# The norm sums of an RWKV-7 recurrence: transposed spreading through TensorE against broadcast reads from a DRAM scratch

## The chip, the cores and the metric

The kernel runs on one core of one Trainium2 chip. The metric is the device time of one execution in microseconds (us). A core has five engines that run side by side, each with its own instruction queue in order: PE (TensorE, matmuls; its weight loads are listed as PEld), DVE (VectorE), ACT (ScalarE), POOL (GpSimd) and SP (SyncE, here only a DMA issuer). PSUM is the memory that matmuls write; SBUF is the working memory with 128 partitions.

## The reference

One step of a one-layer decoder trunk, in fp32, for 1024 prompt tokens and 8 x 8 sample tokens. What matters here is the recurrent branch, with 8 heads of 64 channels:

```python
kk = heads(k * k_k)
kk = kk * rsqrt(sum(kk * kk, over the head) + 1e-12)
...
y, wkv_new = wkv7_scan(state, r, decay, k, v, kk, a)      # delta rule, token by token
mean = mean(y, over the head)
var = mean(square(y - mean), over the head)
y = (y - mean) * rsqrt(var + GN_EPS) * ln_w + ln_b
bonus = sum(rh * kh * r_k, over the head) * vh
y = (y + bonus) * g
```

Each token and head has four such sums over 64 channels: of kk squared, of y, of y squared, and of the bonus. Around it stand one large projection `P = h @ w_in`, a pooling branch, the merge with `w_out`, and an MLP.

## The kernel before, in words

Channels lie on the partitions and the 1088 tokens along the free axis. Two heads share one tile of 128 partitions, so there are four head pairs, f = 0 to 3. A sum over a head is therefore a sum over 64 partitions, which no elementwise engine does. TensorE does it, in two ways:

- `bones`: a matmul with a 128x128 matrix of two blocks of ones gives the head's sum on all its 64 partitions at once. It is used for the mean in `post` (L1204) and in `bonus` (L814), in chunks of 512/288/288 or 364/362/362 tokens.
- `rinv` (L385) and `spread` (L406): nine matmuls of 128 tokens each give the sums with the tokens on partitions (128x2). ACT takes the square root (L396, which loads its table first), DVE the reciprocal (L397), ACT copies the result out to 64 columns per head (L401) and touches Tanh (L403, which loads that table back). `spread` then transposes the 128x128 blocks back, one PE transpose for each block of 128 tokens (L211), and DVE multiplies from PSUM (L720 for kk, L1216 for y).

The sequence for a head pair is `front` (kk's norm and the low-rank terms of decay and `a`), `burst`, `scores` (with `unit` and `bonus`), then `inverse`, `level` and `affine` for the chunks' triangular systems, the chain of chunk states, `sample` and `post` (group norm and gate). `heads` runs `inverse`, `level` and `affine` of f together with a filler: `post` of f-1 followed by `front` of f+1. The inverse is a loop on DVE (L923, L925) that ends with transposes (L933); its result goes through `hv,hv` and `iv,hv` matmuls with an eviction on DVE between them (L954).

The order of PE is written out by hand: generators yield a number of nanoseconds or a condition, and `Pace` puts their matmuls into a dense background stream. In this phase (77 to 752 us of the profile) that stream is the projection `w_in`: 34 blocks of 72 matmuls, each with a 128x128 weight against 362 or 364 tokens. A weight is split into a high and a low half, and each product is three matmuls, written `mm<-hx,whi` and `mm<-hx,wlo`. The splitting (`wlo<-wraw,whi`) is DVE work (L228). The other engines' orders come from a scheduler that estimates times; an engine that reaches an instruction early waits there, and everything behind it waits too. After 752 us stand the merge, the output projection and the MLP, which the change does not touch.

## Time and profile before

| | |
|---|---|
| median of the runs | 1617.38 us (1616.26 to 1618.33, 3 runs) |
| profiled execution | 1622.76 us, span 1621.0 us |
| busy share of the span | PE 97%, PEld 91%, DVE 63%, ACT 45%, POOL 22% |
| phase with the recurrence, 77 to 752 us | PE busy 660.34 of 675.00 us, DVE 389.81, ACT 277.94, POOL 56.98 |
| rest, 752 to 1621 us | PE busy 854.66 of 869.00 us |
| mean granted TensorE clock | 0.989 |

Busy time is the time in which an engine had an instruction under way. Matmuls are pipelined, so their durations in the rows overlap; what a matmul costs the stream is read from the distance between starts, not from its duration. "Idle before, releaser" names what an engine waited for. PEclk is the share of full clock that TensorE was granted.

### The profile page before, as it was taken

How to read it: one execution, taken by the hardware profiler on the slowest of the kernel's cores; microseconds unless marked ns; L12 is line 12 of the kernel's file. 1: busy time of each engine (PE TensorE's matmuls, PEld its weight loads, DVE VectorE, ACT ScalarE, POOL GpSimd, SP SyncE). 2: the span in 40 equal slices, each digit the busy share in tenths (PEclk: the TensorE clock that was granted, in tenths of full speed). 3: DMA queues.
4: the chain of work that ended last, by engine and by line, in shares of the span. 5: the costliest groups of instructions: out<-in, count | busy, mean ns of one | idle time of the engine just before them, and what ended most of it. 6: DMA issues, size and time to landing. Idle time of an engine off the chain costs nothing.

```text
span 1621.0 us, 35482 instructions
## 1 busy us (share of the span) xinstructions
PE 1576.7 (97%) x14331; PEld 1472.5 (91%) x14331; DVE 1020.1 (63%) x1747; ACT 734.6 (45%) x1491; POOL 358.1 (22%) x464
## 2 busy tenths in 40 slices
PE   6999999999999999999999999999999999999997
PEld 3999878997898889879989999999999999999997
DVE  5685574756565636334635587776555677787866
ACT  5543343354334434432325475554445765553323
POOL 3301210020001000101513322333233343521221
PEclk9999999999999999899999999999999999999998
DMA  9334314333413242836874465667666965674313
GB/s 336 108 120 157 134 58 132 108 101 112 152 67 114 90 144 91 296 121 210 328 273 166 143 215 199 205 231 257 223 204 227 321 201 183 199 265 154 101 40 111
DMA packets 123380, 279.43 MB, mean 172 GB/s; under 512 B 16816, under 2 KB 31152, under 8 KB 123216
## 3 DMA queue, kind: packets, MB, share of 16 engines
q1 hardware_dynamic: 107856, 228.52, 41.2%
q0 software_dynamic: 9312, 32.41, 6.0%
q10 hardware_dynamic: 6048, 16.23, 2.9%
q8 instruction: 113, 1.85, 0.5%
q14 instruction: 51, 0.42, 0.1%
HBM read 198.15 MB, written 78.95 MB: 171 GB/s over the span
## 4 chain that ended last, share of the span: by engine, by line
PE 58%; DVE 3%; ACT 3%; issue 3%; DMA 2%; POOL 1%; POOLq 0%; ACTq 0%; SPq 0%; DVEq 0%
PE pr L204 30%; PE mm L204 20%; PE w L204 4%; PE wc L204 3%; DVE hx L1847 1%; DMA wraw<-in_w_out 1%; DMA d_hid<-hx 0%; DMA d_th<-px 0%; ACT whi L227 0%; POOL wlo L228 0%; PE w L211 0%; ACT hx L1770 0%; ACT mr L1770 0%; DVE wlo L228 0%; DMA d_orl<-wt 0%
## 5 line engine op out<-in xcount | busy, mean ns | idle before, releaser
L204 PE MATMUL mm<-hx,whi 128*128 128x362 f32 (+1 forms) x1920 | 509.6, 347 | 0.7 <-ACT px L573 0.7
L204 PEld LDWEIGHTS mm<-hx,whi 128*128 128x128 f32 x1920 | 333.5, 191 | 31.3 <-issue 13.0
L204 PE MATMUL pr<-mr,whi 128*128 128x272 f32 x1792 | 336.2, 287 | 0.2 <-DVE hx L1847 0.2
L204 PE MATMUL mm<-hx,wlo 128*128 128x362 f32 (+1 forms) x960 | 316.4, 330 | 0.0
L204 PEld LDWEIGHTS pr<-mr,whi 128*128 128x128 f32 x1792 | 280.6, 188 | 2.1 <-issue 2.1
L204 PE MATMUL pr<-mr,wlo 128*128 128x272 f32 x896 | 257.8, 288 | 0.0
L227 ACT ACTIVATE whi<-wraw 128x512 fp32r<-128x512 f32 x186 | 116.9, 629 | 204.6 <-PE mm L204 68.1
L228 DVE TENSOR_TENSOR wlo<-wraw,whi 128x512 fp32r<-128x512 f32 x145 | 108.4, 748 | 123.7 <-ACT whi L227 122.8
L204 PEld LDWEIGHTS mm<-hx,wlo 128*128 128x128 f32 x960 | 183.4, 191 | 0.0
L204 PE MATMUL pr<-hx,whi 128*128 128x272 f32 x896 | 168.8, 287 | 2.3 <-ACT hx L1650 0.9
L204 PEld LDWEIGHTS pr<-mr,wlo 128*128 128x128 f32 x896 | 168.6, 188 | 0.0
L204 PE MATMUL mm<-mr,whi 128*128 128x272 f32 (+4 forms) x736 | 152.3, 301 | 0.0
L204 PEld LDWEIGHTS pr<-hx,whi 128*128 128x128 f32 x896 | 140.2, 188 | 3.8 <-ACT hx L1650 1.1
L227 ACT ACTIVATE whi<-wr 128x512 fp32r<-128x512 f32 x138 | 86.3, 627 | 115.3 <-PE pr L204 76.7
L204 PE MATMUL pr<-hx,wlo 128*128 128x272 f32 x448 | 128.9, 288 | 0.0
L204 PEld LDWEIGHTS mm<-mr,whi 128*128 128x128 f32 x736 | 119.2, 188 | 3.0 <-issue 2.5
L204 PE MATMUL mm<-mr,wlo 128*128 128x272 f32 (+4 forms) x368 | 110.1, 299 | 0.0
L228 POOL TENSOR_TENSOR wlo<-wraw,whi 128x512 fp32r<-128x512 f32 x41 | 55.6, 1356 | 216.4 <-ACT whi L227 216.3
L228 DVE TENSOR_TENSOR wlo<-wr,whi 128x512 fp32r<-128x512 f32 x103 | 77.2, 752 | 19.2 <-ACT whi L227 19.2
L204 PE MATMUL pr<-t,whi 128*128 128x272 f32 x448 | 84.7, 287 | 0.7 <-DVE hx L1670 0.7
L204 PEld LDWEIGHTS pr<-hx,wlo 128*128 128x128 f32 x448 | 84.3, 188 | 0.0
L204 PEld LDWEIGHTS pr<-t,whi 128*128 128x128 f32 x448 | 70.1, 188 | 1.8 <-issue 1.8
(467 smaller groups left out, 2714.0 us busy)
## 6 DMA issues: line engine op xcount, KB each, us to landing
wr<-in_w_ff SPq DMA_DIRECT2D x137, 256.0 KB, 3.5
hid<-d_ch POOLq DMA_DIRECT2D x72, 272.0 KB, 3.8
wraw<-in_w_ff SPq DMA_DIRECT2D x71, 256.0 KB, 3.1
wraw<-in_w_in SPq DMA_DIRECT2D x68, 256.0 KB, 2.9
d_ch<-hx SPq DMA_DIRECT2D x52, 272.0 KB, 3.7
hid<-in_w_ada_mlp SPq DMA_DIRECT2D x24, 512.0 KB, 6.2
d_th<-px SPq DMA_DIRECT2D x22, 544.0 KB, 3.0
wt<-d_x SPq DMA_DIRECT2D x20, 544.0 KB, 3.8
```

The costliest lines, as they stand in the source:

```text
L204: return self.nc.tensor.matmul(out, lhsT, rhs, **kw)
L227: nc.scalar.activation(hi, raw, AF.Copy)
L228: (nc.gpsimd if pool else nc.vector).tensor_tensor(lo, raw, hi.bitcast(F32), op=ALU.subtract)
L1847: nc.vector.tensor_tensor(acc, acc, v, op=ALU.add)
```

## The change

1. `bones` goes, except in the last `post`. `strips` puts four matmuls of 272 tokens on the four 32-column strips of TensorE (weights: `hsel`, now 32 wide, two useful columns), so all four write one PSUM bank. `spread_strips` copies the bank to SBUF on ACT, writes it to a DRAM scratch `d_n` in two DMAs and reads it back with two DMAs that repeat a head's row on 64 partitions, all four issued by POOL. This serves `bonus` of all f and the mean in `post` of f = 0 to 2.
2. `rsqrt` takes the place of Sqrt, reciprocal and both table loads: a bit trick and three Newton steps, 11 small DVE instructions.
3. `spread_sums` takes the place of copies and transposes, except in the last `post`: one PE transpose of 18 rows (`kct,rh`), an ACT copy, one DMA to the scratch and four broadcast reads into a tile R, all five on POOL. DVE then multiplies 1088 tokens at a time from SBUF.
4. `front` becomes `keys` and `lora`. A new `between(f)` holds `post` of f-1 with `keys` and `lora` of f+1 in one stream, with fixed times. The last `post()` keeps `bones`, `spread` and the transposes, with `rsqrt`.
5. The constants are split into two tiles, `kct` (kept) and `kc1` (for this phase only).

```diff
-for _name, _w in (("ident", 128), ("hsel", 2), ("bones", 128), ("strict", 64), ("incl", 64), ("strict8", 64), ("incl8", 64),
-                  ("qm", 8), ("icnt", 16), ("one0", 9), ("par", 2), ("m16", 32), ("i32", 32), ("sel", 18)):
+for _name, _w in (("ident", 128), ("one0", 9), ("sel", 18), ("icnt", 16), ("hsel", 32), ("bones", 128), ("strict", 64), ("incl", 64),
+                  ("strict8", 64), ("incl8", 64), ("qm", 8), ("par", 2), ("m16", 32), ("i32", 32)):
     KC[_name] = (_n, _w)
     _n += _w
 NKC = _n
+KEEP = KC["hsel"][0]
...
-    put("hsel", (r // 64) == np.arange(2)[None])
+    put("hsel", (r // 64) == np.arange(32)[None])
...
-        return self.kct[:, o:o + w]
+        return self.kct[:, o:o + w] if o < KEEP else self.kc1[:, o - KEEP:o - KEEP + w]
...
-            self.mm(ps[:, 2 * i:2 * i + 2], x[:, b:b + 128], self.kc("hsel"), start=True, stop=True)
-        r = self.cp.tile([P, 10, 2], F32, tag="rh", bufs=3, name=self.nm("rh"))
-        last, r = r[:, 9, 0:1], r[:, :k, :]
-        f = r.rearrange("p k h -> p (k h)")
-        nc.scalar.activation(f, ps[:, :2 * k], AF.Sqrt, bias=self.eps[:, eps:eps + 1], scale=scale)
-        nc.vector.reciprocal(f, f)
+            self.mm(ps[:, 2 * i:2 * i + 2], x[:, b:b + 128], self.kc("hsel")[:, 0:2], start=True, stop=True)
+        r = self.rsqrt(ps[:, :2 * k], scale, eps).rearrange("p (k h) -> p k h", h=2)
         i = 0
         for x in R:
             m = x.shape[1] // 128
             nc.scalar.activation(x.rearrange("p (k h j) -> p k h j", h=2, j=64), r[:, i:i + m, :].unsqueeze(3).to_broadcast([P, m, 2, 64]), AF.Copy)
             i += m
-        nc.scalar.activation(last, R[-1][:, 0:1], AF.Tanh)
         return [x[:, o:o + 128] for x in R for o in range(0, x.shape[1], 128)]
+    def rsqrt(self, ps, scale, eps):
+        nc, m = self.nc, ps.shape[1]
+        t = self.cp.tile([P, 3, 20], F32, tag="rh", bufs=2, name=self.nm("rh"))
+        x, y, a = (t[:, i, :m] for i in range(3))
+        nc.vector.tensor_scalar(x, ps, scale, EPS[eps], op0=ALU.mult, op1=ALU.add)
+        nc.vector.tensor_scalar(y.bitcast(I32), x.bitcast(I32), -0.5, float(0x5f3759df), op0=ALU.mult, op1=ALU.add)
+        for _ in range(3):
+            nc.vector.tensor_tensor(a, y, y, op=ALU.mult)
+            nc.vector.scalar_tensor_tensor(a, a, -0.5, x, op0=ALU.mult, op1=ALU.mult)
+            nc.vector.scalar_tensor_tensor(y, a, 1.5, y, op0=ALU.add, op1=ALU.mult)
+        return y
+    def strips(self, x):
+        ps = self.ps("w")
+        for j in range(4):
+            self.mm(ps[32 * j:32 * j + 32, :272], self.kc("hsel"), x[:, 272 * j:272 * j + 272], start=True, stop=True, tile_position=(0, 32 * j))
+        return ps[:, :272]
+    def spread_strips(self, ps, m, scale, R):
+        nc, d = self.nc, self.scratch_n()
+        nc.scalar.activation(m, ps, AF.Copy, scale=scale)
+        for h in range(2):
+            nc.gpsimd.dma_start(d[h, :NT].rearrange("(j c) -> j c", j=4), m.rearrange("(j p) c -> j p c", j=4)[:, h])
+        for h, hs in enumerate(HB):
+            nc.gpsimd.dma_start(R[hs], d[h:h + 1, :NT].to_broadcast([64, NT]))
+    def sums(self, x):
+        ps, bl = self.ps("w"), self.blocks(0, NT)
+        v = ps[:, :18].rearrange("p (h k) -> p k h", h=2)
+        for i, b in enumerate(bl):
+            if i and i % 3 == 0:
+                self.pace.fill()
+            self.mm(v[:, i], x[:, b:b + 128], self.kc("hsel")[:, 0:2], start=True, stop=True)
+        return ps[:, :18]
+    def spread_sums(self, r, m, R):
+        nc, d = self.nc, self.scratch_n()
+        ps = self.ps("w")
+        self.tr(ps[:18, :128], r, self.kc("ident"))
+        nc.scalar.activation(m, ps[:18, :128], AF.Copy)
+        nc.gpsimd.dma_start(d.rearrange("h (k c) -> (h k) c", c=128), m)
+        for h, hs in enumerate(HB):
+            nc.gpsimd.dma_start(R[hs, :1024], d[h:h + 1, :1024].to_broadcast([64, 1024]))
+            nc.gpsimd.dma_start(R[hs, 1024:], d[h:h + 1, 1088:1152].to_broadcast([64, 64]))
+    def scratch_n(self):
+        self.nn += 1
+        return self.d_n[self.nn % 2]
+    def spare(self):
+        return self.row(self.p1, "e", 1, w=1112)[:, :NT]
...
-    def front(self, f, got=None):
-        nc, io = self.nc, self.io
-        X = lambda b: lambda: ("X", b) in self.done
+    def keys(self, f, got=None):
+        nc = self.nc
         if got is None:
-            yield X(4 + f)
+            yield lambda: ("X", 4 + f) in self.done
             got = self.fetch(f)
         w2a2, k = got
         kk = self.wt()
         for c0, n in FH:
             nc.scalar.activation(kk[:, c0:c0 + n], k[:, c0:c0 + n], AF.Square, scale=self.par("k_k", f))
+        self.cur = dict(w2a2=w2a2, k=k, kk=kk)
+        yield 9000 if f == 0 else 5500
+        ps = self.sums(kk)
+        r = self.rsqrt(ps, 1.0, 1)
+        yield 3200
+        R = self.spare()
+        self.spread_sums(r, kk[:18, :128], R)
+        nc.vector.scalar_tensor_tensor(kk, k, self.par("k_k", f), R, op0=ALU.mult, op1=ALU.mult)
+    def lora(self, f):
+        nc = self.nc
+        X = lambda b: lambda: ("X", b) in self.done
+        w2a2 = self.cur["w2a2"]
         yield X(12)
         wa = self.wt()
         nc.sync.dma_start(wa, self.d_x[12])
         t1, tha = self.wt(), self.wt()
-        yield self.pace.warm(FW if f else 11000)
-        R = self.rinv(kk, self.blocks(0, NT), 1.0, 1, [kk[:, 0:512], kk[:, 512:1024], t1[:, 0:128]])
-        yield 2500
-        for i, (c0, n) in enumerate(((0, 512), (512, 512), (1024, 64))):
-            ps = self.spread(R[4 * i:4 * i + 4])
-            o = 64 if i == 2 else 0
-            nc.vector.scalar_tensor_tensor(kk[:, c0:c0 + n], k[:, c0:c0 + n], self.par("k_k", f), ps[:, o:o + n], op0=ALU.mult, op1=ALU.mult)
-            yield 800
+        yield 5500
         for c0, n in FP:
             ps = self.ps("w")
             self.mm(ps[:, :n], w2a2[0:64, :], wa[0:64, c0:c0 + n], start=True, stop=True)
...
         yield X(f)
         r = self.wt()
         nc.sync.dma_start(r, self.d_x[f])
-        self.cur = dict(k=k, kk=kk, t1=t1, tha=tha, r=r)
+        self.cur.update(t1=t1, tha=tha, r=r)
...
     def bonus(self, f, d):
         nc, q, v, bv = self.nc, d["q"], d["v"], self.wt()
-        for c0, n in CH:
-            ps = self.ps("w")
-            self.mm(ps[:, :n], self.kc("bones"), q[:, c0:c0 + n], start=True, stop=True)
-            nc.vector.tensor_tensor(bv[:, c0:c0 + n], ps[:, :n], v[:, c0:c0 + n], op=ALU.mult)
-            yield 1000
+        self.spread_strips(self.strips(q), q[:, :272], 1.0, bv)
+        yield 1000
+        nc.vector.tensor_tensor(bv, bv, v, op=ALU.mult)
         nc.sync.dma_start(self.d_bv[f], bv)
...
-    def post(self, f):
+    def between(self, f):
+        nc, p = self.nc, f - 1
+        got = self.fetch(f + 1) if f < 3 else None
+        y = self.wt()
+        for hs, os in zip(HB, HB[::-1]):
+            nc.sync.dma_start(y[hs], self.d_y[p][os])
+        sq = self.wt()
+        keys = self.keys(f + 1, got) if f < 3 else iter(())
+        t = self.pace.t
+        at = lambda x: max(t + x - self.pace.t, 0)
+        next(keys, None)
+        yield at(5000)
+        R = self.spare()
+        self.spread_strips(self.strips(y), sq[:, :272], -1.0 / 64, R)
+        nc.vector.tensor_tensor(y, y, R, op=ALU.add)
+        for c0, n in FH:
+            nc.scalar.activation(sq[:, c0:c0 + n], y[:, c0:c0 + n], AF.Square)
+        yield at(6500)
+        next(keys, None)
+        yield at(10000)
+        next(keys, None)
         sg = self.wt()
         nc.sync.dma_start(sg, self.d_x[13])
-        if not last:
-            for hs, os in zip(HB, HB[::-1]):
-                nc.sync.dma_start(y[hs], self.d_y[f][os])
+        g2 = self.sm.tile([P, P], F32, tag="sw", bufs=2, name=self.nm("sw"))
+        nc.sync.dma_start(g2, self.io["g2"][:, p * 128:(p + 1) * 128])
+        yield at(15500)
+        for c0, n in CH:
+            ps = self.ps("w")
+            self.mm(ps[:, :n], g2, sg[:, c0:c0 + n], start=True, stop=True)
+            nc.scalar.activation(sg[:, c0:c0 + n], ps[:, :n], AF.Copy)
+            yield 500
+        yield at(19500)
+        r = self.rsqrt(self.sums(sq), 1.0 / 64, 2)
+        yield 3200
+        R = self.spare()
+        self.spread_sums(r, sq[:18, :128], R)
+        nc.sync.dma_start(sq, self.d_bv[p])
+        nc.vector.scalar_tensor_tensor(y, y, self.par("ln_w", p), R, op0=ALU.mult, op1=ALU.mult)
+        nc.vector.scalar_tensor_tensor(y, y, self.par("ln_b", p), sq, op0=ALU.add, op1=ALU.add)
+        nc.vector.tensor_tensor(y, y, sg, op=ALU.mult)
+        hi, lo = sq.bitcast(F32R), y.bitcast(F32R)
+        nc.scalar.activation(hi, y, AF.Copy)
+        nc.vector.tensor_tensor(lo, y, hi.bitcast(F32), op=ALU.subtract)
+        nc.sync.dma_start(self.d_or[0][p], hi.bitcast(F32))
+        nc.sync.dma_start(self.d_or[1][p], lo.bitcast(F32))
+        self.done.add(("or", p))
+        if f < 3:
+            yield 9000
+            yield from self.lora(f + 1)
...
+    def post(self):
+        nc, f = self.nc, 3
+        y = self.y3
+        g2 = self.sm.tile([P, P], F32, tag="sw", bufs=2, name=self.nm("sw"))
+        nc.sync.dma_start(g2, self.io["g2"][:, 384:512])
+        sg = self.wt()
+        nc.sync.dma_start(sg, self.d_x[13])
...
             def fill():
-                if f == 0:
-                    self.got = self.fetch(1)
-                yield from self.post(f - 1) if f else self.ada_fill()
-                if f < 3:
-                    yield from self.front(f + 1, self.got)
+                if f:
+                    yield from self.between(f)
+                else:
+                    got = self.fetch(1)
+                    yield from self.ada_fill()
+                    yield from self.keys(1, got)
+                    yield from self.lora(1)
...
-        yield from self.both(self.sample(3, d), self.post(3))
+        yield from self.both(self.sample(3, d), self.post())
...
+            self.d_n = [dp.tile([2, 1152], F32, name=f"d_n{i}") for i in range(2)]
...
+        self.kc1 = self.pxp.tile([P, NKC - KEEP], F32, name="kc1")
+        nc.gpsimd.dma_start(self.kc1, io["kc"][:, KEEP:])
```

Some places show the new order. The first is on DVE, at the end of the inverse of f = 1. Before, the loop (`tt`), its evaluation (`iv`, L929) and its transposes (L931, L933) are followed by a weight split and the mean of y:

```order
L925 TENSOR_REDUCE tt<-hv_3717 128x2x15
L929 TENSOR_SCALAR iv_3851<-tt,kct 128x32x16
L931 STREAM_TRANSPOSE hv_3855<-iv_3851 128x16x32
L933 STREAM_TRANSPOSE iv_3854<-iv_3851 128x16x32 x2
L228 TENSOR_TENSOR wlo_3820<-wraw_3817,whi_3819 128x512
L1205 SCALAR_TENSOR_TENSOR wt_3722<-wc_3844,wt_3722 128x512
```

Now the end of that loop's transposes stands among the Newton steps (`rh`, L412 to L414) for kk of f = 2; behind them come y plus its mean (L1241), a weight split, kk times R (L770) and only then the eviction between `hv,hv` and `iv,hv` (L1012):

```order
L991 STREAM_TRANSPOSE iv_3866<-iv_3863 128x16x32
L413 SCALAR_TENSOR_TENSOR rh_3788<-rh_3788 128x18
L414 SCALAR_TENSOR_TENSOR rh_3788<-rh_3788 128x18
L412 TENSOR_TENSOR rh_3788<-rh_3788 128x18
L413 SCALAR_TENSOR_TENSOR rh_3788<-rh_3788 128x18
L414 SCALAR_TENSOR_TENSOR rh_3788<-rh_3788 128x18
L412 TENSOR_TENSOR rh_3788<-rh_3788 128x18
L413 SCALAR_TENSOR_TENSOR rh_3788<-rh_3788 128x18
L414 SCALAR_TENSOR_TENSOR rh_3788<-rh_3788 128x18
L1241 TENSOR_TENSOR wt_3691<-wt_3691,e_3747 128x1088
L231 TENSOR_TENSOR wlo_3887<-wraw_3884,whi_3886 128x512
L770 SCALAR_TENSOR_TENSOR wt_3695<-wt_3688,part,e_3835 128x1088
```

The norm of kk for the next head pair has moved from behind the filler's `post` to the end of the current inverse, and the eviction of the inverse's own chain now stands behind a multiplication that needs R.

The second place is on PE, where the norm of y of f = 0 is spread during the level of f = 1. Before, nine transposes (L211) stand in the stream, in groups of four, four and one:

```order
L211 MATMUL wc_4210<-kct,wt_3729 128x128 x4
L204 MATMUL mm_3908<-hx_360,whi_3894 128x362
L204 MATMUL mm_3908<-hx_361,whi_3894 128x362
L204 MATMUL mm_3908<-hx_360,wlo_3895 128x362
L204 MATMUL mm_4251<-hx_346,whi_4085 128x364
L204 MATMUL mm_4251<-hx_347,whi_4085 128x364
L204 MATMUL mm_4251<-hx_346,wlo_4086 128x364
L204 MATMUL mm_4252<-hx_346,whi_4085 128x362
L204 MATMUL mm_4252<-hx_347,whi_4085 128x362
L204 MATMUL mm_4252<-hx_346,wlo_4086 128x362
L211 MATMUL wc_4260<-kct,wt_3729 128x128 x4
L211 MATMUL w_4266<-kct,sw_3723 128x128
```

Now one transpose (L214, of the 18 rows `rh`) stands there; the same form for kk of f = 2 is shown, 15 stream matmuls behind the last of the sums:

```order
L207 MATMUL mm_3814<-hx_350,whi_3646 128x362
L207 MATMUL mm_3814<-hx_351,whi_3646 128x362
L207 MATMUL mm_3814<-hx_350,wlo_3647 128x362
L214 MATMUL w_3836<-kct,rh_3788 18x128
L207 MATMUL mm_3815<-hx_350,whi_3646 128x362
L207 MATMUL mm_3815<-hx_351,whi_3646 128x362
```

PE waits at that transpose until `rh` is done on DVE, and the stream behind it waits with it.

63 lines of the change are left out of this document (23 added, 40 removed).

## The prediction, made before the changed kernel ran

> **What bounds the kernel now.** I read the busy shares first, then the windows of the two phases. In the fence: the page's line of busy times, and the rows of windows (stretch, length, busy time of each engine, granted clock, DMA share, GB/s).
>
> ```profile
> span 1621.0 us, 35482 instructions
> PE 1576.7 (97%) x14331; PEld 1472.5 (91%) x14331; DVE 1020.1 (63%) x1747; ACT 734.6 (45%) x1491; POOL 358.1 (22%) x464
> 77.00:752.00 675.00, 660.34 (x7428) 584.88 (x7427) 389.81 (x721) 277.94 (x656) 56.98 (x107) 0.98 0.38 126
> 506.50:513.30 6.80, 6.19 (x59) 5.28 (x54) 5.35 (x9) 2.71 (x7) 0.00 (x0) 0.50 0.65 215
> 660.10:670.40 10.30, 10.30 (x95) 10.22 (x95) 0.27 (x1) 6.01 (x12) 2.86 (x3) 0.50 0.74 278
> ```
>
> The reader is to see that PE sets the time: in the recurrence's phase it is idle 675.00 − 660.34 = 14.7 us, and the other engines have room. So PE work taken out of this phase is worth its full time, and a wait of PE costs its full time. Two stretches ran at half clock (0.50); they cost about 6.8/2 = 3.4 and 10.3/2 = 5.1 us. A change of under 0.2% (3.2 us) could not be told from none.
>
> **PE work.** What an instruction costs the stream is read from starts. In the PE timeline (start, duration, instruction), the mean by `bones`, four transposes, four column strips and the sums stand among stream matmuls:
>
> ```profile
> 127.27 0.33 PE L204 MATMUL mm<-hx,wlo 128*128 128x364 f32 x1
> 127.44 0.77 PE L204 MATMUL w<-wt,kct 128*128 128x362 f32 x2
> 127.77 0.78 PE L204 MATMUL mm<-hx,whi 128*128 128x362 f32 x2
> 128.38 0.32 PE L204 MATMUL mm<-hx,wlo 128*128 128x362 f32 x1
> 128.54 0.49 PE L204 MATMUL mm<-hx,whi 128*128 128x362 f32 x2
> ...
> 85.30 0.33 PE L204 MATMUL mm<-hx,wlo 128*128 128x362 f32 x1
> 85.47 0.60 PE L211 MATMUL wc<-kct,wt 128*128 128x128 f32 x4
> 85.82 0.58 PE L204 MATMUL mm<-hx,whi 128*128 128x364 f32 x2
> 86.24 0.33 PE L204 MATMUL mm<-hx,wlo 128*128 128x364 f32 x1
> ...
> 170.00 0.33 PE L204 MATMUL mm<-hx,wlo 128*128 128x364 f32 x1
> 170.26 1.07 PE L204 MATMUL wc<-wt,sT 128*32 128x512 f32 x8
> 171.26 0.60 PE L204 MATMUL mm<-hx,whi 128*128 128x362 f32 x2
> 171.69 0.33 PE L204 MATMUL mm<-hx,wlo 128*128 128x362 f32 x1
> ```
>
> From 128.38 to 128.54 one stream matmul takes 0.165 us. From 127.27 to 128.38 there are three of them (0.495) and one `bones` of 362 tokens (two passes), which therefore costs 0.61; scaled by columns, 1088 tokens cost 1.83. Removed are seven sets of 1088 tokens (four `bonus`, three `post`): −12.8 us. The four transposes cost 86.24 − 85.30 − 0.495 = 0.445, 0.111 each; 63 go (nine each for four kk and three y): −7.0.
>
> Added are seven groups of four strips. The row of strips at 170.26 has four of 512 tokens (eight passes) and costs 171.69 − 170.00 − 0.495 = 1.195. For 272 tokens it lies between 1.195 × 272/512 = 0.635 and 1.195 itself; I take 0.79, nearer to the lower end since the columns are what falls. Seven: +5.5 (4.4 to 8.4). One transpose for nine, seven times at about 0.12: +0.8. The sums of 128x2 stay. Net on PE: −12.8 − 7.0 + 5.5 + 0.8 = **−13.5** (−14.6 to −10.6).
>
> The Trainium skill ("TensorEngine Tiling (Array Packing)", Key Properties) says that column tiles run in parallel and that a change of the tiling mode drains the array. By it, four strips of 272 tokens cost one pass pair, 0.61 × 272/362 = 0.46 us, and the drains. The trace agrees in kind: four strips of 512 cost 1.195, against 0.86 for one `bones` of 512 by the scaling above, so 0.33 is left for drains, and 0.46 + 0.33 gives the same 0.79.
>
> **Waits that go.** Around 502 us the norm of y ran on ACT, and PE waited for a pooling eviction behind it. Timelines of ACT, DVE and PE (in brackets idle time and releaser), then of PE at 659 us:
>
> ```profile
> 500.22 1.28 ACT L396 ACT_TABLE_LOAD   x1
> 503.19 0.29 ACT L401 ACTIVATE sw<-rh 128x128 f32<-128x128 f32 x1
> 503.38 0.54 ACT L683 ACTIVATE d<-w,part 128x364 fp32r<-128x364 f32 x1
> 503.96 0.60 DVE L684 SCALAR_TENSOR_TENSOR px<-w,part,d 128x364 fp32r<-128x364 f32 x1 [1.86 <-ACT d L683]
> 504.61 0.77 PE L204 MATMUL w<-px,plw 128*128 128x298 f32 x2 [1.85 <-DVE px L684]
> 507.93 0.48 PE L211 MATMUL w<-kct,wt 128*128 128x128 f32 x1 [0.47 <-DVE px L684]
> 659.86 0.38 PE L204 MATMUL wc<-kct,wt 128*128 128x2 f32 x2 [0.96 <-issue]
> ```
>
> The table load begins a run of Sqrt and copies up to 503.48; L683 stands behind it, L684 behind L683, PE behind L684. Without them −1.85 and −0.47, and the wait inside the sums at 659.86 (−0.96) belongs to the last `post`, whose Sqrt goes too: −3.3 together. The half clock from 506.50 follows on that gap, so I let it go as well: −3.4. The one from 660.10 I leave, since the last `post` stays. ACT, POOL and SP work that goes or comes is worth nothing by itself, as PE is the bound.
>
> **Waits that come.** The 11 Newton instructions are on the path only where DVE is late. For kk of f = 2 they stand behind the inverse of f = 1, and for f = 3 behind that of f = 2. PE's `uv,ak` is the common mark ahead of both (PE and DVE timelines, f = 1 then f = 2):
>
> ```profile
> 311.13 1.15 PE L204 MATMUL wc<-uv,ak 64*64 64x64 f32 x32
> 323.21 1.92 DVE L933 STREAM_TRANSPOSE iv<-iv 128x512 f32<-128x512 f32 x2
> 324.96 0.68 DVE L228 TENSOR_TENSOR wlo<-wraw,whi 128x512 fp32r<-128x512 f32 x1
> 308.21 0.17 DVE L923 TENSOR_TENSOR hv<-hv,tt 128x18 f32<-128x18 f32 x1
> ...
> 467.19 1.15 PE L204 MATMUL w<-uv,ak 64*64 64x64 f32 x32
> 477.79 1.92 DVE L933 STREAM_TRANSPOSE iv<-iv 128x512 f32<-128x512 f32 x2
> 657.68 0.50 PE L204 MATMUL wc<-kct,wt 128*128 128x2 f32 x4
> 658.04 0.41 PE L204 MATMUL mm<-hx,whi 128*128 128x362 f32 x1
> ```
>
> f = 1: L933 ends 325.13 − 311.13 = 14.0 us after `uv,ak`; a weight split (0.68) and 11 small instructions at the 0.17 of the 128x18 row (1.9) bring `rh` to 16.5. PE arrives at its transpose after `uv,ak` (1.1), 48 stream matmuls (7.9), pooling of 1088 tokens (1.83), strips (0.79) and nine sums at two passes each, by the four passes from 657.68 to 658.04 some 0.11 a pass (2.0): 13.6. Wait: **+2.8**. f = 2: L933 ends at 12.5; with splits and Newton steps `rh` is at about 15.7. PE has no pooling but 57 matmuls: 1.1 + 9.4 + 0.79 + 2.0 = 13.3. Wait: **+2.4**. Since a gap of 1.85 us was followed by a half-clock stretch, I add the shortest one, half of 3.4 us, after each: **+3.4** (0 to 6.8).
>
> Then R. POOL's rows are issue (busy, mean ns) and landing (KB, us from issue to landing); behind them a 1088-wide DVE row and the `hv,hv` matmuls on PE:
>
> ```profile
> L672 POOL DMA_DIRECT2D plw<-in_pool_w x4 | 2.2, 557 | 30.6 <-PE wc L204 17.6 <-PE w L204 12.9
> plw<-in_pool_w POOLq DMA_DIRECT2D x4, 64.0 KB, 2.4
> hid<-d_ch POOLq DMA_DIRECT2D x72, 272.0 KB, 3.8
> psm<-in_spool POOLq DMA_DIRECT2D x4, 60.0 KB, 4.2
> hx<-d_cl POOLq DMA_DIRECT2D x8, 272.0 KB, 8.8
> L1239 DVE TENSOR_TENSOR wt<-wt,wt 128x1088 fp32r<-128x1088 f32 x3 | 3.9, 1286 | 3.4 <-ACT wt L1238 3.4
> 486.54 1.29 PE L204 MATMUL wc<-hv,hv 32*32 32x32 f32 x128
> ```
>
> No row shows a small scratch write or a repeating read, so I bound them: the write lands in 2.4 to 4.2, the last read in 3.8 to 8.8. Five issues at 0.557. I take the low ends (small sizes): transpose and copy 0.6, write 2.4, four issues 2.2, read 3.8, so R is there 9.0 us after `rh`, at most 15.8. While DVE waits at L770, the eviction L1012 behind it waits, and PE's `iv,hv` behind that. For f = 2 `iv,hv` stands 48 matmuls (7.9), two low-rank chunks (1.2) and `hv,hv` (1.3) behind the transpose, about 10.5 us; R plus L770 (1088 wide, 1.3) and L1012 (512 wide like the split, 0.7) is 11, and queueing adds a little: a wait of 0 to 7, **+1.3**. For f = 1 there are 51 matmuls and a full set of low-rank chunks: 0. For f = 0, L770 stands ahead of evictions of the affine part: 0 to 4, **+0.5**. The second norm of f = 1 has only six matmuls between sums and transpose (1.0, and `iv,hv`) against 1.9 of Newton steps and one L1019 transpose between them: **+1.5**. What queues on POOL behind the write's landing (the chain's products with `end`, L1017) is late by up to those 2.4 us; POOL is busy 57 of 675 us, so I cost it at 0. New waits: 2.8 + 2.4 + 1.3 + 0.5 + 1.5 + 3.4 = **+11.9**.
>
> The recurrence also ends earlier against the stream, since fixed times take the place of conditions. Its last part then meets another stretch of weights and DMA; nothing in the profile prices that: 0, from −5.1 (the half clock at 660.10 gone) to +5.1 (one more like it).
>
> **Sum.** −13.5 − 3.3 − 3.4 + 11.9 = −8.3 us. The profiled execution (1622.76, span 1621.0) lies 5.4 above the median; I take the difference as the same in both. 1617.4 − 8.3 = **1609 us**.
>
> **Rivals.**
> - New waits mostly hidden. If DVE's loop is ordered a little earlier against PE, the Newton waits and their half-clock stretches go (−8.6), and the stretch at 660 may go too (−5.1): 1595 to 1600. For it: idle PE is only 14.7 us in 675, so this order has hidden most such waits. Against: the rows above put `rh` behind L933.
> - The gain is eaten. Newton waits at both places, R about 3 us later in f = 0 and f = 2, one more half-clock stretch (3.4): −8.3 + 6 + 3.4 = +1, so 1614 to 1620.
> - Slower: the scratch route is slow. With the upper ends, R comes 6.8 us later; at f = 0, 1, 2 L770 holds L1012 that much longer, and each gap brings half of 3.4 us of half clock: 3 × 8.5 = 25.5, so 1634. It decides from 4 us later on, (4 + 1.7) × 3 = 17 against the 8.3 and 3.2. For it: 8.8 us is a POOL row from this core. Against: 3.8 is the median of 72.
>
> The Trainium skill ("SBUF — State Buffer", SBUF: two separate sides) has a rule for this rival: a DMA that POOL issues needs its descriptors written through a port that some DVE operations lock, so it is late while DVE is busy. POOL's issues here took 557 ns in a phase where DVE was busy 58% of the time, which does not show it; I leave it inside that rival's chance.
>
> **How the numbers follow.** Forecast (1602 to 1614) 0.50; waits hidden (1593 to 1602) 0.20; gain eaten 0.18; slower 0.12. A time under 1614.2 is faster by over 0.2%: 0.50 + 0.20 and a little of the third, 0.72. From 1614.2 to 1620.6: 0.16. Above: 0.12. The range for 8 in 10 runs from 1595 to 1621.
>
> **What would show it.** Right: fewer PE instructions in 77 to 752, about 13 us less PE work; no table loads but four; PE waiting 2 to 3 us for `rh` in f = 1 and f = 2; R landing 9 us after `rh`. Wrong: half-clock stretches at new places, L770 waiting for a DMA over 12 us with PE idle behind L1012, strips above 1 us, or the DVE rows of the inverse later than here.

## The result and the profile after

The changed kernel takes 1632.88 us (median, 1630.78 to 1635.57) against 1617.86: a ratio of 1.0094 with a 95% interval of 1.0074 to 1.0115, 15 us slower. The forecast was 1609 us, with a range of 1595 to 1621. The rival "the scratch route is slow" had 1634 and a chance of 0.12.

The page's lines of busy times, and one row of windows for the same stretch of work in each trace (from 31 us to the first matmul of the phase after the projection; before, then after):

```profile
span 1632.7 us, 35541 instructions
PE 1570.6 (96%) x14289; PEld 1462.4 (90%) x14289; DVE 1032.7 (63%) x1803; ACT 704.4 (43%) x1445; POOL 391.8 (24%) x528
```

```profile
31.00:912.60 881.60, 865.16 (x8895) 777.59 (x8896) 507.78 (x912) 356.45 (x787) 131.76 (x200) 0.99 0.44 149
```

```profile
31.00:923.60 892.60, 859.07 (x8853) 767.17 (x8853) 518.11 (x969) 325.38 (x742) 165.67 (x263) 0.98 0.47 156
```

The stretch became 11.0 us longer (of 11.7 in the span), though PE was busy 6.1 us less: idle PE went from 16.4 to 33.5 us. (The profiled execution of the kernel before, 1622.76 us, lay 4.9 above its median, so the two traces show 11.7 of the 15 us.) The busy time has to be parted once more, since at half clock an instruction counts as busy for longer. I added up the busy time that lies in half-clock stretches and took half of it as lost: 11.64 us before, 17.43 after. What is left is the work proper: 865.16 − 11.64 = 853.5 us before and 859.07 − 17.43 = 841.6 after. So the account is: work **−11.9**, idle PE **+17.1**, half clock **+5.8**, together +11.0. The half is a round estimate: the stream matmuls start 0.302 us apart in these stretches (median) and 0.166 outside them, which makes the loss 0.45 of the busy time; the account is then −11.3, +17.1 and +5.2.

The work came out close to the forecast −13.5. Its most doubtful term was the strips. The PE timeline after:

```profile
311.72 0.32 PE L207 MATMUL mm<-hx,wlo 128*128 128x362 f32 x1
311.98 0.67 PE L207 MATMUL w<-wt,kc 128*32 128x272 f32 x8
312.57 0.60 PE L207 MATMUL mm<-hx,whi 128*128 128x364 f32 x2
313.01 0.33 PE L207 MATMUL mm<-hx,wlo 128*128 128x364 f32 x1
```

Four strips cost 313.01 − 311.72 − 0.495 = 0.795 us, where 0.79 was taken. The Trainium skill ("TensorEngine Tiling (Array Packing)", Key Properties) has tiles running in parallel and a drain at a change of mode. This row agrees in kind: by the forecast's 0.46 us for one strip, four in turn would take an estimated 4 × 0.46 = 1.84, and all four took 0.795.

The idle time is read from the waits of PE (waited for: us in total, times, longest):

```profile
PE w L214 <- DVE rh L414: 6.7, 2, 4.2
PE wc L207 <- DMA wt<-d_x: 5.3, 1, 5.3
PE wc L207 <- DVE ra L1089: 2.6, 1, 2.6
PE w L207 <- DVE px L739: 2.4, 1, 2.4
PE wc L207 <- DVE hv L1012: 2.1, 1, 2.1
PE mm L207 <- ACT px L679: 1.9, 1, 1.9
...
PE mm L207 <- ACT px L661: 1.5, 1, 1.5
...
PE wc L214 <- DVE rh L414: 0.6, 1, 0.6
```

The first and the last row are the waits for the Newton steps, 7.2 us (4.25, 2.41 and 0.56) where 2.8 + 2.4 + 1.5 were forecast. DVE and PE at f = 1:

```profile
320.50 1.03 DVE L991 STREAM_TRANSPOSE iv<-iv 128x512 f32<-128x512 f32 x1
...
322.88 0.18 DVE L414 SCALAR_TENSOR_TENSOR rh<-rh 128x18 f32<-128x18 f32 x1
```

```profile
323.11 0.38 PE L214 MATMUL w<-kct,rh 128*18 128x128 f32 x1 [4.25 <-DVE rh L414]
```

The last transpose of the inverse ends at 321.53, seven more steps start after that, and PE has stood for 4.25 us.

What the forecast had at 1.8 us was the way of R. The largest single gap, in f = 2, shows all of it; from the timelines of PE, ACT, POOL, DVE and SP:

```profile
504.94 0.28 PE L214 MATMUL w<-kct,rh 128*18 128x128 f32 x1
529.40 2.08 PE L207 MATMUL wc<-wt,sw 64*128 64x512 f32 x4 [5.26 <-DMA wt<-d_x]
505.06 1.21 ACT L1035 ACTIVATE hv<-w 32x512 f32<-32x512 f32 x2 [6.33 <-PE w L207]
506.29 0.27 ACT L448 ACTIVATE wt<-w 18x128 f32<-18x128 f32 x1
505.10 2.14 POOL L1075 TENSOR_TENSOR hv<-kct,end 64x512 f32<-64x512 f32 x2 [7.32 <-PE w L207]
507.19 0.55 POOL L449 DMA_DIRECT2D d_n<-wt  x1
509.37 0.54 POOL L451 DMA_DIRECT2D e<-d_n  x1 [1.63 <-issue]
...
510.95 0.53 POOL L452 DMA_DIRECT2D e<-d_n  x1
517.69 1.35 DVE L1264 SCALAR_TENSOR_TENSOR wt<-wt,part,e 128x1088 f32<-128x1088 f32 x1 [9.89 <-DMA e<-d_n]
524.30 1.29 DVE L1266 TENSOR_TENSOR wt<-wt,wt 128x1088 f32<-128x1088 f32 x1
525.62 0.32 SPq L779 DMA_DIRECT2D wt<-d_x  x1
```

The roots are transposed at 504.94. The copy waits on ACT behind L1035, the write on POOL behind L1075, four reads are issued one after the other, and R is used at 517.69, 12.7 us after the transpose and 6.7 after the last read was issued. DVE has stood still for 9.89 us; what has queued there meanwhile runs between the tail's instructions, so that L1266 ends only at 525.6. Only then is a buffer free for the low-rank part's input (L779), which lands at 529.4. PE waits 5.26 us.

The same tail behind y's R holds PE at f = 1 and f = 3 too. In the waits of DVE and the PE timeline:

```profile
DVE wt L1264 <- DMA e<-d_n: 24.9, 3, 10.7
364.98 0.43 PE L207 MATMUL mm<-hx,whi 128*128 128x362 f32 x1 [1.92 <-ACT px L679]
674.88 0.34 PE L207 MATMUL wc<-uv,ab 128*64 128x64 f32 x4 [2.62 <-DVE ra L1089]
```

DVE stood 24.9 us in all at the three places where y meets R (L1264). At 365 ACT had stood 4.62 us at the tail's L1268, and the stream's eviction (L679) came behind it; at 675 DVE did the chain's eviction (L1089) only behind L1264 to L1266. So 5.26 + 1.92 + 2.62 = 9.8 us of PE's idle time stand behind y's R, 7.2 at the roots and 2.1 at L1012: 19.1 of the 33.5 us.

### The profile page after: what moved, and what is told of

Its sections match the earlier page's. It is cut to its first block, busy times and chain, and to the rows that moved or that the text cites. A ratio compares the mean times of both kernels' runs of the same rounds, so it can differ in the third digit from the quotient of the medians.

```text
span 1632.7 us, 35541 instructions
## 1 busy us (share of the span) xinstructions
PE 1570.6 (96%) x14289; PEld 1462.4 (90%) x14289; DVE 1032.7 (63%) x1803; ACT 704.4 (43%) x1445; POOL 391.8 (24%) x528
## 4 chain that ended last, share of the span: by engine, by line
PE 62%; DVE 5%; issue 3%; DMA 3%; ACT 2%; POOL 1%; DVEq 0%; POOLq 0%; ACTq 0%; SPq 0%
PE pr L207 31%; PE mm L207 22%; PE w L207 5%; PE wc L207 4%; DMA wraw<-in_w_out 1%; DMA e<-d_n 1%; DVE hx L1942 1%; DMA d_th<-px 1%; POOL wlo L231 0%; DVE hv L981 0%; ACT whi L230 0%; DVE wlo L231 0%; ACT hx L1865 0%; DVE tt L983 0%; DVE hx L2111 0%
## 5 line engine op out<-in xcount | busy, mean ns | idle before, releaser
L207 PEld LDWEIGHTS mm<-hx,whi 128*128 128x128 f32 x1920 | 335.4, 192 | 37.8 <-issue 19.3
```

Source lines behind the costliest of these rows:

```text
L207: return self.nc.tensor.matmul(out, lhsT, rhs, **kw)
```

## The experiments

The columns of work, idle PE and half clock are worked out for each profiled execution as above; between kernels whose PE instructions are the same, the work differs by up to 3.8 us (839.0 to 842.8), so smaller differences in it mean little. One execution stands for each kernel there, and it can lie some us from the median (a_pool's took 1636.5 us, the median is 1631.6). The kernel before was run again beside each; its medians lay between 1616.19 and 1619.64 us, so a difference of two medians of different sessions is good to a few us, and the ratio is the safer figure.

| kernel | median, us | ratio to before (95%) | work | idle PE | half clock |
|---|---|---|---|---|---|
| before | 1617.9 | | 853.5 | 16.4 | 11.6 |
| after | 1632.9 | 1.0094 (1.0074 to 1.0115) | 841.6 | 33.5 | 17.4 |
| b_rsqrt | 1619.6 | 1.0022 (1.0009 to 1.0036) | 853.9 | 16.1 | 8.2 |
| b_bonus | 1625.1 | 1.0051 (1.0033 to 1.0070) | 853.1 | 23.8 | 10.1 |
| b_pool | 1618.0 | 1.0000 (0.9985 to 1.0014) | 851.8 | 16.8 | 10.4 |
| b_pool2 | 1616.2 | 0.9998 (0.9986 to 1.0011) | 852.5 | 16.7 | 6.8 |
| b_sp | 1620.3 | 1.0017 (1.0000 to 1.0033) | 852.5 | 19.0 | 8.1 |
| a_later | 1635.6 | 1.0105 (1.0074 to 1.0137) | 839.0 | 26.6 | 29.7 |
| a_lora | 1633.3 | 1.0102 (1.0067 to 1.0137) | 840.2 | 28.6 | 20.2 |
| a_sq | 1632.5 | 1.0087 (1.0065 to 1.0109) | 840.6 | 28.6 | 18.5 |
| a_pool | 1631.6 | 1.0077 (1.0053 to 1.0102) | 842.6 | 35.1 | 16.9 |
| a_sp | 1634.8 | 1.0113 (1.0082 to 1.0144) | 842.5 | 33.1 | 18.6 |
| a_two_reads | 1645.2 | 1.0168 (1.0145 to 1.0191) | 842.8 | 39.8 | 21.1 |
| a_newton6 | 1654.7 | 1.0208 (1.0181 to 1.0235) | 842.1 | 50.4 | 23.1 |
| a_bones | 1654.1 | 1.0229 (1.0195 to 1.0262) | 843.5 | 39.2 | 30.4 |
| a_stretch | 1632.4 | 1.0102 (1.0077 to 1.0128) | 840.6 | 31.7 | 17.1 |
| a_gate | 1627.8 | 1.0060 (1.0040 to 1.0081) | 842.8 | 23.3 | 16.1 |
| a_gate_sp2 | 1627.7 | 1.0060 (1.0034 to 1.0086) | 840.8 | 26.8 | 21.7 |

### One part at a time on the kernel before

**b_rsqrt**

```diff
-        nc.scalar.activation(f, ps[:, :2 * k], AF.Sqrt, bias=self.eps[:, eps:eps + 1], scale=scale)
-        nc.vector.reciprocal(f, f)
+        r = self.rsqrt(ps[:, :2 * k], scale, eps).rearrange("p (k h) -> p k h", h=2)
...
-        nc.scalar.activation(last, R[-1][:, 0:1], AF.Tanh)
```

> The kernel before with one part of the change: the 11 DVE instructions (bit trick and Newton steps) in place of Sqrt, reciprocal and both table loads; transposes, bones and the order stay. If the table loads and Sqrt were behind the waits at 502 and 659 us, those waits go and the kernel gains 2 to 7 us. If the Newton steps themselves are the trouble (DVE late), it loses 2 us or more: nine sets of about 2.3 us each on DVE.

0.2% slower (0.09 to 0.36%), so the gain of 2 to 7 us did not come; it is a loss of about 3 us, as the rival had it, though not shown to be the Newton steps. The forecast had 3.3 us of waits going with the table loads, and the half clock at 506. That half clock is gone in the trace (and another of 6.8 us has come at 79), but the idle time is not: waits of 1.02 and 0.72 us remain around 505, and a new one of 1.62 has come at 209, where PE waits for the copies behind the steps. The profiled execution, 1617.02 us, is the fastest of the ten, so its account does not hold the loss; where that lies is not shown. PE's waits in this kernel:

```profile
PE wc L206 <- ACT S L1097: 4.5, 4, 2.7
PE wc L213 <- ACT wt L399: 2.3, 2, 1.6
```

**b_bonus**

```diff
-        for c0, n in CH:
-            ps = self.ps("w")
-            self.mm(ps[:, :n], self.kc("bones"), q[:, c0:c0 + n], start=True, stop=True)
-            nc.vector.tensor_tensor(bv[:, c0:c0 + n], ps[:, :n], v[:, c0:c0 + n], op=ALU.mult)
-            yield 1000
+        self.spread_strips(self.strips(q), q[:, :272], 1.0, bv)
+        yield 500
+        nc.vector.tensor_tensor(bv, bv, v, op=ALU.mult)
```

> The kernel before with one part of the change: bonus by four column strips, an ACT copy and the scratch route, the constants in two tiles, 0.5 us instead of 1 in the order behind it. Nothing on PE waits for its result, so by the theory that PE work counts in full and only waits spoil the change it gains 4 x (1.83 - 0.79) = 4.2 us. By the rival that the strips cost more than taken, or that POOL's DMAs disturb the rest, it gains nothing or loses.

0.5% slower, with 7.4 us more idle PE, though nothing on PE needs the bonus. Timelines of POOL, DVE and PE:

```profile
437.09 0.52 POOL L422 DMA_DIRECT2D wt<-d_n  x1 [0.81 <-DMA d_n<-wt]
447.28 1.29 DVE L838 TENSOR_TENSOR wt<-wt,wt 128x1088 f32<-128x1088 f32 x1 [4.71 <-issue]
448.49 1.22 DVE L677 SCALAR_TENSOR_TENSOR px<-d,px 128x1024 f32<-128x1024 f32 x1
449.75 0.17 DVE L678 COPY px<-zf 128x7 f32<-128x7 f32 x1
450.02 1.55 PE L205 MATMUL w<-px,plw 128*128 128x364 f32 x2 [6.14 <-issue]
```

The second read is issued at 437.6 and its data are used at 447.28. DVE stands at the product (L838) for 4.71 us, the pooling's last steps (L677, L678) stand behind it, and PE, which needs these, stands for 6.14.

The expected 4.2 us of PE work did not show either. The strips cost what was taken (0.795 us at 431), but the work of the four kernels with this bonus (b_bonus, b_pool, b_pool2, b_sp) is only 0.4 to 1.7 us below that of the kernel before. Many later matmuls stand in another order there; what took the rest stays open.

**b_pool**: the same, with one word changed.

```diff
-        nc.vector.tensor_tensor(bv, bv, v, op=ALU.mult)
+        nc.gpsimd.tensor_tensor(bv, bv, v, op=ALU.mult)
```

> The kernel before with bonus by strips and scratch (as in the run that lost 0.5%), and one edit on top: the product of the broadcast sum with v is made by POOL instead of DVE. The same DMAs at the same places, but DVE no longer waits for them. By the theory that the loss is DVE standing at that product while the pooling behind it makes PE wait (6.14 us at 444 us and 3.50 at 521), it gains 6 to 12 us against that run and ends at or below the kernel before (1612 to 1618). By the rival that the scratch DMAs disturb the other loads themselves, it stays at 1622 to 1627.

7.1 us less than b_bonus and level with the kernel before: the 6.14 us gap is gone. The reads land as late as in b_bonus (a median of 8.9 us against 8.6), and POOL now stands at the product. This shows the mechanism at this place: with the DMAs unchanged, the loss was DVE standing in order at data not yet landed. A second gap of 3.50 us, which b_bonus has at 521, stayed.

**b_pool2**: also `nc.sync.dma_start(plw, ...)` for `nc.gpsimd`.

> The kernel before with bonus by strips and its product on POOL, and the pooling weights loaded by SP instead of POOL. In the run before, PE still waited 3.50 us at 513 us for a pooling matmul whose weights queue on POOL behind that product. By the theory of POOL's in-order queue that wait goes with the half clock behind it: 1611 to 1616. By the rival that it was the pooling data and not the weights, unchanged at 1616 to 1620.

The 3.50 us gap stayed again, so my explanation of it by POOL's queue is wrong, and the rival had the time. DVE and PE there:

```profile
514.30 0.16 DVE L678 COPY px<-zf 128x15 f32<-128x15 f32 x1
514.57 0.54 PE L205 MATMUL w<-px,plw 128*128 128x364 f32 x1 [3.50 <-issue]
```

PE starts 0.11 us after the pooling's last step on DVE, so it was the data and not the weights. DVE had been busy without a gap since 499.14, with the pooling's steps and the tail of y's norm in turn. The time is that of the kernel before.

**b_sp**: b_bonus with `nc.sync.dma_start(R[hs], ...)` for the reads.

> The kernel before with bonus by strips and the product on DVE (the run that lost 0.5%), with the two broadcast reads issued by SP instead of POOL. By the theory that the reads are late because other transfers of the same moment share the engines of the DMA, they still land after 7 us or more and the time stays within 3 us of that run (1622 to 1628). By the rival that POOL's issue is the trouble (its descriptors wait while DVE is busy), they land within 4.5 us, and the time falls by 4 us or more.

DMA issues (KB each, median us to landing) of b_bonus and of b_sp:

```profile
wt<-d_n POOLq DMA_DIRECT2D x8, 272.0 KB, 8.6
```

```profile
wt<-d_n SPq DMA_DIRECT2D x8, 272.0 KB, 5.5
```

The time fell by 4.8 us and the reads land 3.1 us sooner, yet not in 4.5. So the issuing engine is part of it and not all: 5.5 us remain beside the other transfers of that moment. The Trainium skill ("SBUF — State Buffer", SBUF: two separate sides) says that descriptors written by POOL can wait for DVE, and that issuing elsewhere avoids it; the 3.1 us fit that, but no run kept DVE idle to show that DVE is the cause.

### The changed kernel, one thing at a time

**a_two_reads**: each long read of R issued twice (`for _ in range(2):`).

> The changed kernel with a suspected cost doubled: each of the two long broadcast reads of the inverse roots is issued twice, with the same data. By the theory that R's lateness is on PE's path (through L770, L1264 and the buffer that they hold), each R is 2 to 4 us later and four or five of the seven places add that: 8 to 20 us more. By the rival that the loss is only the Newton steps and half clock, 0 to 3 us more.

12.3 us more, as the lateness of R has it: 1.8 us for each of the seven spreads. R was used 2.3 to 4.9 us later behind its roots at all seven places. The run delays the R of kk and that of y together and doesn't tell them apart.

**a_newton6**: `range(6)` for `range(3)` in `rsqrt`.

> The changed kernel with a suspected cost doubled: six Newton steps instead of three, nine more small DVE instructions (about 1.9 us) in each of the nine sets. By the theory that the roots are on PE's path only where they stand behind the inverse or right ahead of their transpose (kk in f = 1 and f = 2, y in f = 1), the waits for rh grow by 1.9 us each, from 7 to about 13, and the time by 4 to 9 us with the half clock. By the rival that every set is on the path, 15 us or more; if the roots are hidden, 0 to 2.

21.8 us more; the rival had this. PE's waits for `rh`:

```profile
PE w L214 <- DVE rh L414: 20.8, 4, 8.4
PE wc L214 <- DVE rh L414: 6.0, 3, 2.8
```

Seven places wait now, 26.8 us instead of 7.2. At f = 2 the wait grew by 6 us for 1.9 us of steps, since the scheduler now put y's mean among the steps, and that waits for its own scratch read (DVE timeline):

```profile
490.57 1.29 DVE L1241 TENSOR_TENSOR wt<-wt,e 128x1088 f32<-128x1088 f32 x1 [2.94 <-DMA e<-d_n]
491.78 0.17 DVE L414 SCALAR_TENSOR_TENSOR rh<-rh 128x18 f32<-128x18 f32 x1
```

So hardly any of the nine sets has slack on DVE, and the two costs add up where a late read stands in front of late roots: 2.41 + 1.9 + 2.94 + 1.29 = 8.5, where 8.4 were measured.

**a_later**: `yield at(14500)` for `yield at(10000)`.

> The changed kernel with one number changed: the transpose of kk's norm 4.5 us later in the order (14500 for 10000). By the theory of waits the 4.25 and 2.41 us at the transposes for rh go, and L1012, which now stands ahead of L770 on DVE, no longer waits (2.1); with a half-clock stretch or two this gives 7 to 12 us back. By the rival that the scratch route is the loss wherever it stands, R is late for the low-rank part instead and the time stays within 3 us.

Idle PE fell by 7 us (both waits at kk's transposes went), and nothing was gained; the time stayed within the rival's 3 us. The half clock took 12.3 us more. Part of this is one stretch of it, in a row of windows:

```profile
646.50:663.60 17.10, 16.88 (x241) 16.38 (x242) 3.34 (x14) 6.71 (x14) 4.64 (x5) 0.50 0.06 18
```

**a_lora**: `yield 15000` for `yield 9000` ahead of the low-rank part.

> The changed kernel with one number changed: the low-rank part begins 15 instead of 9 us behind the group norm's spreading. If the 5.26 us wait at 524 us is there because its input's buffer comes free only after R has been used, that wait goes: 4 to 8 us back with the half-clock stretch behind it. By the rival that the stall only moves to the next head pair's burst, which needs the low-rank part, the time stays within 3 us.

The 5.26 us wait went, other waits took 3.5 us of it at the next pooling and 3.4 at 669, and the time stayed: the rival.

**a_sq**: y's mean is broadcast into `sq` instead of `R`.

> The changed kernel with one edit: the mean of y is broadcast into the tile of the squares instead of the one R tile, so kk's R need not wait for y's sum. In f = 2 the four reads of R were issued 4.2 us after the write since they wrote the tile that y's sum was still read from. By the theory of R's lateness, L770 comes up to 4 us earlier in f = 1 and f = 2 and the wait at L1012 (2.1 us) goes: 2 to 6 us back. By the rival (lateness hidden) within 2 us.

The wait at L1012 went and idle PE fell by 5 us, half clock rose by 1.1 (a stretch of it runs on past the end of the window); the median is the same, within the rival's 2 us.

**a_pool**: bonus product and k with R on POOL.

> The changed kernel with two products moved from DVE to POOL: the bonus with v and k with R (two POOL instructions). DVE then waits for R only at L1264 and at y's mean. By the theory of DVE's in-order waits the gaps behind L770 (2.1 us at L1012, and what follows it) and the pooling waits go: 4 to 10 us back against the changed kernel. The waits for rh and the 5.26 us wait stay. By the rival that POOL, busier and in order too, holds the next spread and the pooling's loads, nothing or a loss.

1.3 us less, inside the spread of the runs, which is the rival's "nothing". The gap behind L1012 went, and a new wait of 5.4 us came at 524 for a chain's eviction on DVE; in DVE's order this stands behind the product of y with R, which waited 11.72 us for its DMA.

**a_sp**: all broadcast reads issued by SP.

> The changed kernel with one edit: all broadcast reads issued by SP instead of POOL; the scratch writes stay on POOL. By the theory that R's lateness is the loss, the waits behind R (5.26 us for the buffer, 2.1 at L1012, 1.9 and 1.5 at the projection's evictions) shrink and the time falls by 4 to 10 us; the 6.7 us of waits for rh stay. By the rival that SP, in order too, then holds the projection's weights while it waits for the scratch writes, nothing or a loss.

No gain, as the rival had it: the reads of R land 0.6 us sooner (3.9 for 4.5 us), the wait for the buffer shrank from 5.3 to 1.8, and the others grew by as much.

**a_bones**: the bonus as before the change.

> The changed kernel with one part undone: bonus by bones and DVE from PSUM, no scratch. PE work rises by 4.2 us. By the theory that the bonus's broadcast makes DVE wait here as it did in the kernel before (6.14 and 3.50 us there), the waits saved outweigh it: 0 to 6 us faster than the changed kernel. By the rival that in this order the bonus is hidden and only the norms cost, 3 to 5 us slower.

21 us slower, outside both expectations. The matmuls and waits of the bonus moved the whole later order, with 13 us more of half clock; the run doesn't tell what the bonus is worth here.

### Taking the waits away by order

**a_stretch**

```diff
-        yield at(10000)
+        yield at(14500)
-        yield at(15500)
+        yield at(18500)
-        yield at(19500)
+        yield at(25000)
-        yield 3200
+        yield 4500
-            yield 9000
+            yield 16000
-        yield 9000 if f == 0 else 5500
+        yield 11500 if f == 0 else 5500
```

with the edits of a_sq, the bonus product on POOL and the pooling weights by SP.

> The changed kernel with its waits taken away by order alone: kk's transpose 4.5 us later, the gate's matmuls 3 and the second sums 5.5 us later, 1.3 us more ahead of the second transpose, the low-rank part 7 us later, the first head's norm 2.5 us later; besides the mean of y into the tile of squares, the bonus's product on POOL, the pooling weights loaded by SP. PE does the same work. By the theory that PE work is saved as forecast (12 to 13.5 us) and the loss is waits and the half clock behind them, idle PE falls from 33 to 20 us or less and the time to 1608 to 1620. By the rival that the work itself costs more than the matmuls removed, the time stays above 1625 with little idle PE.

No gain, and neither expectation: the time is above 1625, but PE is still idle for 31.7 us. Most waits for the roots are gone, and one of 8.05 us at 665 has come. ACT's timeline there:

```profile
670.37 1.11 ACT L1267 ACTIVATE wt<-wt 128x1088 fp32r<-128x1088 f32 x1 [6.97 <-DVE wt L1265]
...
672.60 0.81 ACT L661 ACTIVATE px<-mm 128x364 f32<-128x364 f32 x2
```

Here it is ACT that stands in order: L1267 belongs to the tail behind R, and the eviction of the dense stream (L661) queues behind it.

**a_gate**: the same, with the gate's matmuls 13 us of order behind the transpose, and the tail made to need them.

```diff
-        nc.vector.scalar_tensor_tensor(y, y, self.par("ln_w", p), R, op0=ALU.mult, op1=ALU.mult)
-        nc.vector.scalar_tensor_tensor(y, y, self.par("ln_b", p), sq, op0=ALU.add, op1=ALU.add)
-        nc.vector.tensor_tensor(y, y, sg, op=ALU.mult)
+        nc.vector.tensor_tensor(R, R, sg, op=ALU.mult)
+        nc.vector.scalar_tensor_tensor(sq, sq, self.par("ln_b", p), sg, op0=ALU.add, op1=ALU.mult)
+        nc.vector.scalar_tensor_tensor(y, y, self.par("ln_w", p), R, op0=ALU.mult, op1=ALU.mult)
+        nc.vector.tensor_tensor(y, y, sq, op=ALU.add)
```

> As the stretched version of the changed kernel, but with the group norm's tail made to depend on the gate's matmuls, which now stand 13 us of order behind the transpose of the roots: R is multiplied by the gate first, so DVE's order has the chain's evictions (L1088) ahead of everything that needs R. One more 1088-wide DVE instruction per head. By the theory that DVE and ACT standing at R held PE (8.05 us at 665, 3.5 at 366, 3.0 at 517), those gaps go and the time falls by 8 to 18 us against the stretched version, to 1614 to 1624. By the rival that the scratch transfers themselves or the sparse phases cost the time, within 4 us of it.

The gaps at 366, 517 and 665 are gone, idle PE fell by 8.4 us and the time by 4.6, less than expected. So the tail behind R was a part of the loss; 23.3 us of idle PE and 16.1 of half clock are left against 16.4 and 11.6 before.

**a_gate_sp2**: a_gate with the reads by SP and the first head's old time.

> The stretched version with the gate ahead of R's uses, the broadcast reads issued by SP, and the first head's norm back at its old place (where it waited 2 us for the squares instead of 3.4 for the roots). By the theory, idle PE falls to about that of the kernel before (16 us) and the 11 us of PE work saved show: 1608 to 1618. By the rival that the half clock stays as long as PE's sparse parts are cut by any gap of 1 to 3 us, 1620 to 1628.

The rival: no gain over a_gate. Idle PE and half clock are above those of a_gate, with waits at other places. The longest, 4.89 us at 504 for L1019, is again DVE in its order, this time at kk's R:

```profile
498.77 1.35 DVE L770 SCALAR_TENSOR_TENSOR wt<-wt,part,e 128x1088 f32<-128x1088 f32 x1 [9.03 <-DMA e<-d_n]
...
503.20 0.71 DVE L1019 STREAM_TRANSPOSE hv<-wc 128x512 f32<-128x512 f32 x1
```

No version was faster than the kernel before; b_pool2 and b_pool are level with it.

## Why the prediction was wrong

The forecast had −8.3 us, the stretch measured +11.0. Of the 19.3 us between them, idle PE has 11.9 (+5.2 forecast by the waits that come and go, +17.1 measured), half clock 5.8, work 1.6.

- **The PE work** was right in sum: −11.9 against −13.5, the strips at 0.795 against 0.79. Whether it counted in full in the time is not shown: no version of the changed kernel got its waits down to those of the kernel before, and with the bonus alone (b_bonus, b_pool, b_pool2, b_sp) less work was saved than the strips should give.
- **"Waits that come", the Newton steps:** right in mechanism and in sum (7.2 against 6.7 us; 4.25, 2.41 and 0.56 against 2.8, 2.4 and 1.5). f = 1 was low: three evictions of the pooling (L739, 0.6 us each) stand behind `uv,ak` among the inverse's steps, where one did before, and 11 steps take 2.3 us, not 1.9. (The four passes from 657.68 to 658.04 are 0.09 us each, not 0.11, which alone makes both waits 0.4 longer. The 1.5 for y was too high.)
- **"Then R"** is the step that failed, with a total of 1.8 us. I followed only one thing behind R, the eviction L1012 (2.1 us where 1.3 were taken), and had not looked at the tail behind y's R at all. On it hang the buffer of the low-rank input (5.26 us), by ACT in its order the projection's evictions (1.92 us at 363), and by DVE in its order the chain's (2.62 us at 672): 9.8 us that stood at nothing. a_two_reads shows that the lateness of R counts, a_gate that the tail behind y's R is a part of it, and b_pool shows the same mechanism at the bonus.
- **How late R is:** the low ends that I took were near the medians of the landings (2.5 us for the scratch write where 2.4 was taken, 4.5 for a long read where 3.8 was), and kk's R in f = 1 was used 9.0 us after its roots, as forecast. What the sum left out is the queueing: for y, 15.1 to 16.6 us passed from roots to use, since the copy stands in order on ACT and the write on POOL, and the reads land late (6.7 us from the last issue to the use at f = 2).
- **Bonus and mean** were costed at PE work alone, though DVE has to wait for their reads as well. At the bonus's product it stood 8.7 us in all (three places); whether that cost PE time in the changed kernel's order is not shown.
- **"Waits that go":** −3.3 and −3.4 for the Sqrt and its table loads did not show in the time: b_rsqrt alone is 0.2% slower. In the changed kernel the three waits and the half clock at 506 are gone from their places, but a wait of 2.36 us for the same kind of pooling eviction (L739) has come at 385, and half clock came elsewhere.
- **Half clock:** I had +3.4 − 3.4 = 0; it was +5.8, and between 6.8 and 30.4 us in the kernels tried. Most of its stretches begin in or right behind a gap, so a gap tends to cost more than its length, by an amount that I could not forecast.
- **The rivals:** the outcome lies at "slower", with its mechanism (L770 and the late landing) only in part: DVE stood at L770 for 4.0 us at most, and the price came from y's tail, DVE's and ACT's order, and the half clock. Its point of decision, R 4 us later than the low ends, was passed for y. With the middle of the bounds instead of the low ends (R 3.4 us later), the forecast would have been near the kernel before, by the rival "the gain is eaten".

What stays open: the other 14.4 us of idle PE one by one (before, it was 16.4 in all); why some waits only move when they are taken away one by one (a_later, a_lora, a_sq and a_sp all kept the time); and how much of the loss is half clock. No version got back more than about a third of the 15 us (a_gate, 5.1), and no run took half clock away by itself.

## What to carry to other kernels

Work taken off the bounding engine is worth its time only if no engine that it waits for is made to stand in order at something slow. Before a matmul is traded for a round trip through DRAM, list for each engine on the way what stands behind the waiting instruction, to the end of the chain of its result, not only the first consumer; and give the product to an engine on which nothing urgent queues (b_pool: 7.1 us for one word). A wait found in such a dense order should be priced with its half-clock stretch, and removing waits one at a time may show nothing, as the next in line takes their place.

## What the runs showed of the hardware

- A read that repeats one DRAM row on 64 partitions (272 KB) landed after a median of 8.6 us when POOL issued it and 5.5 when SP did, at the same place in the same kernel; in the changed kernel the medians were 5.6 and 4.9.
- Half clock is not bound to an idle PE. It came in stretches of 3.4 us and multiples of it, and lasted 17.1 us in the stretch of a_later shown above, in which PE was busy 16.88 us. In the changed kernel each stretch of the recurrence's phase began in a gap of PE of 0.6 to 5.3 us or within 2.5 us behind it, while the gaps of 1.50 us at 112 and 2.62 at 672 had none; in a_stretch one began at 647.1 with no gap over 0.5 us in the 8 us ahead.
- A chain of dependent DVE instructions on 128x18 elements runs at 0.21 us a step (322.23, 322.44, 322.67, 322.88 in the changed kernel), so 11 of them take 2.3 us (500.32 to 502.62 there), not the 1.9 that durations of 0.17 add up to.
